# The scheduler's times come from the timeline simulation; the traced program stays the same

## The chip, the cores and the metric

One core of a Trainium2 chip runs the kernel. The metric is the device time of one launch in microseconds. Before the change the median of three runs is 2724.34 us, the lowest 2723.51 and the highest 2725.11.

A core has engines with in-order instruction streams of their own: PE (TensorE, matmuls, with a second stream for loading weights, PEld), DVE (VectorE), ACT (ScalarE), POOL (GpSimd) and SP, which here issues DMAs. They meet at semaphores. Matmuls write into PSUM, which this kernel divides into eight banks of 128 x 512 fp32.

## What is computed

A decoder trunk of four layers over 512 tokens of 1024 channels, all in fp32. Layer i has a token mixer (Gated DeltaNet, HGRN2, GLA, Gated DeltaNet) and a SwiGLU channel mixer:

```
for i in range(DEPTH):                       # DEPTH = 4
    kind, j = i % N_MIXERS, i // N_MIXERS
    if kind == 0:   m = gated_deltanet(x, gdn_w_in[j], ..., gdn_w_out[j])
    elif kind == 1: m = hgrn2(x, hgrn_w_in[j], lb_all[i], hgrn_norm_w[j], hgrn_w_out[j])
    else:           m = gla(x, gla_w_in[j], ..., gla_w_out[j])
    x = layer_norm(DN_ALPHA * x + m, mix_ln_g[i], mix_ln_b[i])
    x = layer_norm(DN_ALPHA * x + swiglu(x, ffn_w_in[i], ffn_w_down[i]), ffn_ln_g[i], ffn_ln_b[i])
```

Each mixer projects x (`x @ w_in`), runs a chunked linear recurrence over the tokens for each head (8 heads of 128 in GDN and HGRN2; 4 heads of 128 keys and 256 values in GLA), normalizes, gates and projects back. GDN has a causal convolution over 4 tokens, L2-normalized q and k, and a triangular solve in each chunk; HGRN2 and GLA have a decay for each key channel, which the kernel builds up level by level.

## The kernel before, in words

Channels lie on the 128 partitions and the 512 tokens along the free axis. A projection makes 128 channels by 512 tokens: eight blocks of 128 input channels, each with three matmuls of 512 columns (`mm3`, L183 to L185), since every fp32 operand is split into a high and a low part. The tiles are called pj (projection), vp (a block of values by tokens) and dn (output and down projections). Weights come by DMA (wraw); ACT casts the high part (whi, L144) and DVE subtracts it for the low one (wlo, L147). There are six buffers each for whi and wlo: a cast waits until the matmuls of six splits earlier have read theirs. Four PSUM banks (`acc`) take projections, four (`mx`) everything else.

The mixers add many small steps, in which one engine waits for another:

- GDN, `gdn` from L552: per half of the heads, decays (gb, L650 to L657), then for each pair of heads the projections of q and k, the convolution (`conv`, a scaling on ACT at L627, three multiply-adds on DVE at L631; for the first pair it reads a copy `raw`, for the second the PSUM bank of pj itself), silu on ACT (L637), products of k with k and q (kk, L689), transposes (tp, L505), squares on ACT (L702). Then `solve` (L820 to L909), which inverts the triangular blocks from 16 to 32 to 64 and 128 rows: L859 and L865, L877 and L891, L902 and L908 are its matmuls, with copies and transposes on ACT and DVE between; then four steps of the state (ch, L776 to L794).
- HGRN and GLA: `decay_head` (L944) builds a head's matrix am by levels. Two calls of `quad` (matmuls sc at L927) are followed by three levels of 16, 32 and 64 tokens: matmuls (L965), copies into am on ACT (L967), and two products on DVE (L972, L973) that give the next level its q and k. Then transposes (tp), a copy kt, and `decay_chains` (L983): state products su (L990), outputs ob (L995, L1003).
- `finish` normalizes a group of heads by the squares that ACT sums (L513), with the small DVE operations of `rsqrt` (L135 to L139) and a product (L533); `flush` transposes it for the output projection (ytp, L543) and multiplies by the gate (L550).

The code writes these steps down in an order that already weaves small steps with projections. The order on each engine is then made by the framework's scheduler when the program has been traced: it goes through time, and at each moment gives every engine the instruction that stands first in the traced order among those whose inputs and buffers are ready. When something is ready follows from times that the scheduler has for each instruction. Only two parts set PE's order by hand: the loading of x, and the layer norm behind a projection (`down_norm`, L355). The changed line is in `kernel`, where the context is made in which `trunk` is traced.

## Time and profile before

| | |
|---|---|
| median of three runs | 2724.34 us (2723.51 to 2725.11) |
| the profiled execution's own time | 2725.05 us |
| its span | 2723.3 us |
[...]
| instructions | 37712 |
| busy: PE, DVE, ACT, POOL | 2664.1, 1520.1, 1060.2, 90.3 us |
| read from HBM, written | 240.61 MB, 8.39 MB |

A row of a group of instructions has the line, engine, operation and tiles, the count, the busy time and the mean in ns of one, and the idle time of the engine just before them with what ended it. A PE busy time overlaps from one matmul to the next, so the spacing of matmuls is read from the number in a stretch rather than from the mean of one. An fp32 matmul of small tiles has two records, a transpose one.

### The profile page before, as it was taken

How to read it: one execution, taken by the hardware profiler on the slowest of the kernel's cores; microseconds unless marked ns; L12 is line 12 of the kernel's file. 1: busy time of each engine (PE TensorE's matmuls, PEld its weight loads, DVE VectorE, ACT ScalarE, POOL GpSimd, SP SyncE). 2: the span in 40 equal slices, each digit the busy share in tenths (PEclk: the TensorE clock that was granted, in tenths of full speed). 3: DMA queues.
4: the chain of work that ended last, by engine and by line, in shares of the span. 5: the costliest groups of instructions: out<-in, count | busy, mean ns of one | idle time of the engine just before them, and what ended most of it. 6: DMA issues, size and time to landing. Idle time of an engine off the chain costs nothing.

```text
span 2723.3 us, 37712 instructions
## 1 busy us (share of the span) xinstructions
PE 2664.1 (98%) x15279; PEld 2224.7 (82%) x15279; DVE 1520.1 (56%) x3155; ACT 1060.2 (39%) x2123; POOL 90.3 (3%) x176
## 2 busy tenths in 40 slices
PE   9999999999999999999999999999999999999998
PEld 8787888888877778888887878888887887888886
DVE  7676653333777786323366676323378586833235
ACT  5464442122544434222254634222255554422220
POOL 1000000001000000000000000000010100000000
PEclk9999999999999999999999999999999999999999
DMA  5213223223221332223321332232322132322321
GB/s 158 63 48 101 86 94 108 93 93 109 93 78 47 97 120 93 93 98 103 110 95 63 96 122 93 93 104 97 109 94 78 48 101 78 101 93 93 99 87 62
DMA packets 199678, 251.43 MB, mean 92 GB/s; under 512 B 9082, under 2 KB 152576, under 8 KB 199504
## 3 DMA queue, kind: packets, MB, share of 16 engines
q1 hardware_dynamic: 195152, 237.29, 27.1%
q0 software_dynamic: 4352, 11.73, 1.5%
q8 instruction: 120, 1.97, 0.3%
q14 instruction: 54, 0.44, 0.1%
HBM read 240.61 MB, written 8.39 MB: 91 GB/s over the span
## 4 chain that ended last, share of the span: by engine, by line
PE 81%; DVE 12%; ACT 4%; issue 2%; DMA 1%; POOL 0%; SPq 0%; DVEq 0%; ACTq 0%; POOLq 0%
PE pj L183 16%; PE pj L184 16%; PE pj L185 16%; PE dn L183 7%; PE dn L184 7%; PE dn L185 7%; DVE am L932 2%; DVE wlo L147 1%; ACT junk L702 1%; PE sc L965 1%; PE kk L689 1%; DVE qk L631 1%; PE xtp L221 1%; PE vp L183 1%; PE vp L184 1%
## 5 line engine op out<-in xcount | busy, mean ns | idle before, releaser
L183 PE MATMUL pj<-xTl,whi 128*128 128x512 f32 (+1 forms) x2472 | 925.9, 375 | 0.0
L184 PE MATMUL pj<-xTh,whi 128*128 128x512 f32 (+1 forms) x2472 | 922.3, 373 | 0.0
L185 PE MATMUL pj<-xTh,wlo 128*128 128x512 f32 (+1 forms) x2472 | 922.1, 373 | 0.0
L144 ACT CAST whi<-wraw 128x1024 fp32r<-128x1024 f32 x400 | 420.1, 1051 | 1179.4 <-PE pj L184 796.1
L147 DVE TENSOR_TENSOR wlo<-wraw,whi 128x1024 fp32r<-128x1024 f32 x400 | 487.9, 1222 | 633.5 <-ACT whi L144 633.2
L183 PEld LDWEIGHTS pj<-xTl,whi 128*128 128x128 f32 x2472 | 468.6, 190 | 78.0 <-issue 0.7
L185 PEld LDWEIGHTS pj<-xTh,wlo 128*128 128x128 f32 x2472 | 468.2, 189 | 77.7 <-issue 0.5
L184 PEld LDWEIGHTS pj<-xTh,whi 128*128 128x128 f32 x2472 | 468.5, 190 | 77.0 <-issue 0.7
L453 DVE TENSOR_TENSOR sg<-sg,pj 128x512 f32<-128x512 f32 x88 | 60.5, 687 | 247.4 <-PE pj L185 247.0
L183 PE MATMUL dn<-wlo,hhi 128*128 128x512 f32 x416 | 161.8, 389 | 0.0
L184 PE MATMUL dn<-whi,hhi 128*128 128x512 f32 x416 | 161.8, 389 | 0.0
L185 PE MATMUL dn<-whi,hlo 128*128 128x512 f32 x416 | 161.8, 389 | 0.0
L352 DVE SCALAR_TENSOR_TENSOR x<-x,dn 128x512 f32<-128x512 f32 x96 | 64.5, 684 | 69.1 <-PE dn L185 69.1
L185 PEld LDWEIGHTS dn<-whi,hlo 128*128 128x128 f32 x416 | 78.1, 188 | 16.3
L183 PEld LDWEIGHTS dn<-wlo,hhi 128*128 128x128 f32 x416 | 78.1, 188 | 16.2
L184 PEld LDWEIGHTS dn<-whi,hhi 128*128 128x128 f32 x416 | 78.1, 188 | 16.2
L183 PE MATMUL dn<-wlo,nt 128*128 128x512 f32 x224 | 87.5, 390 | 0.0
L184 PE MATMUL dn<-whi,nt 128*128 128x512 f32 x224 | 87.1, 389 | 0.0
L185 PE MATMUL dn<-whi,nt 128*128 128x512 f32 x224 | 87.1, 389 | 0.0
L183 PE MATMUL dn<-wlo,xTh 128*128 128x512 f32 x192 | 77.5, 404 | 2.8 <-ACT xTh L468 2.8
L184 PE MATMUL dn<-whi,xTh 128*128 128x512 f32 x192 | 75.9, 395 | 0.0
L185 PE MATMUL dn<-whi,xTl 128*128 128x512 f32 x192 | 74.9, 396 | 0.0
(388 smaller groups left out, 3310.7 us busy)
## 6 DMA issues: line engine op xcount, KB each, us to landing
wraw<-in_ffn_w_in SPq DMA_DIRECT2D x88, 1024.0 KB, 5.1
wraw<-in_ffn_w_down SPq DMA_DIRECT2D x40, 1024.0 KB, 5.0
wraw<-in_gdn_w_in SPq DMA_DIRECT2D x32, 1024.0 KB, 5.8
wraw<-in_hgrn_w_in SPq DMA_DIRECT2D x16, 1024.0 KB, 5.8
wraw<-in_gla_w_in SPq DMA_DIRECT2D x12, 1024.0 KB, 5.2
wraw<-in_gdn_w_out SPq DMA_DIRECT2D x8, 1024.0 KB, 5.1
xd<-x SPq DMA_DIRECT2D x24, 256.0 KB, 2.0
x<-xd SPq DMA_DIRECT2D x24, 256.0 KB, 6.5
```

What stands on the lines that cost most here:

```text
L144: nc.scalar.copy(hi, raw)
L147: (eng or nc.vector).tensor_tensor(lo, raw, hi.bitcast(F32), ALU.subtract)
L183: mm(out, ah, bl, start=start, stop=False)
L184: mm(out, ah, bh, start=False, stop=False)
L185: self.last_mm = mm(out, al, bh, start=False, stop=stop).ins
L221: nc.tensor.transpose(ps[:, k], src[:, k * P:(k + 1) * P], self.ident)
L352: self.nc.vector.scalar_tensor_tensor(s, s, alpha, ps, ALU.mult, ALU.add)
L453: nc.vector.tensor_tensor(s, s, pss[2 + j], ALU.mult)
L631: V.scalar_tensor_tensor(dst[:, T - n:], ps[:, :n], wc(t), dst[:, T - n:], ALU.mult, ALU.add)
L689: mm(pk[:, i], k[:, sl], src[:, sl], start=True, stop=True)
L702: S.activation(junk, ptk[:, i], AF.Square, accum_out=ss[:, n_src, lh * NT + i:lh * NT + i + 1])
L932: V.copy_predicated(av[:, c, js], self.lmask[b][:, gs], pm[:, c, gs])
```

## The change

One argument is added. With it the scheduler takes the times by which it chooses from the timeline simulation. The traced program, its tiles, pools and operations are the same; what changes is the order of instructions on each engine, and with it which buffer is free when.

```diff
@@ -1224,7 +1224,7 @@
     out = nc.dram_tensor("out_0", (1, T, D), F32, kind="ExternalOutput").ap()
-    with tile.TileContext(nc) as tc:
+    with tile.TileContext(nc, schedule_with_timeline_sim=True) as tc:
         trunk(tc, aps, out)
     r = run_bass_kernel_spmd(nc, [arrays], core_ids=[0])
```

About 2080 of 13389 instructions of PE, 950 of 3157 of DVE and 460 of 1869 of ACT stand elsewhere among the rest. Nearly all of them are in the four mixers. In PE's order the runs of projection matmuls (pj, vp, dn) that smaller matmuls of the mixers break number 308 before and 198 after.

In the orders below the numbers behind a name tell tiles apart: whi_109 is one cast weight, kk_66 one bank.

Before, on PE, at the first pair of heads of the first GDN layer (kk, the products of k with k and q, and tp, transposes):

```order
L184 MATMUL pj_102_705<-xTh_84,whi_100_701 128x512
L689 MATMUL kk_66_553<-qk_59_507 128x128 x4
L689 MATMUL kk_67_559<-qk_55_492,qk_59_507 128x128 x4
L505 MATMUL tp_69_566<-ident_86,qk_59_507 128x128 x4
L505 MATMUL tp_74_583<-ident_86,qk_55_492 128x128 x4
L185 MATMUL pj_102_705<-xTh_84,wlo_101_703 128x512
L689 MATMUL kk_79_596<-qk_64_544 128x128 x4
L689 MATMUL kk_80_602<-qk_57_499,qk_64_544 128x128 x4
L183 MATMUL pj_102_705<-xTl_85,whi_100_701 128x512
```

After, the same place:

```order
L185 MATMUL pj_111_777<-xTh_84,wlo_110_775 128x512
L689 MATMUL kk_66_553<-qk_59_507 128x128 x4
L689 MATMUL kk_67_559<-qk_55_492,qk_59_507 128x128 x4
L505 MATMUL tp_69_566<-ident_86,qk_59_507 128x128 x4
L505 MATMUL tp_74_583<-ident_86,qk_55_492 128x128 x4
L689 MATMUL kk_79_596<-qk_64_544 128x128 x4
L689 MATMUL kk_80_602<-qk_57_499,qk_64_544 128x128 x4
L505 MATMUL tp_82_609<-ident_86,qk_64_544 128x128 x4
L505 MATMUL tp_87_626<-ident_86,qk_57_499 128x128 x4
L183 MATMUL pj_166_979<-xTl_85,whi_157_961 128x512
```

kk and tp, which stood inside the projection pj_102, now stand in one block behind all four projections of the second pair of heads (pj_98 to pj_111), with no matmul of a projection between them.

Before, on ACT, ahead of the silus (L637) that kk_66 and its neighbours need:

```order
L627 ACTIVATE qk_64_544<-raw_65_545,cw_38_405 128x512
L637 ACT_TABLE_LOAD
L637 ACTIVATE qk_55_492<-qk_55_492 128x512
L637 ACTIVATE qk_57_499<-qk_57_499 128x512
L144 CAST whi_162_971<-wraw_161_969 128x1024
L637 ACTIVATE qk_59_507<-qk_59_507 128x512
L637 ACTIVATE qk_64_544<-qk_64_544 128x512
L697 ACTIVATE kd_68_565<-tp_69_566,gcols_39_407 128x128 x2
L702 ACTIVATE junk_70_575,ssqk_53_490<-tp_69_566 128x128
```

After, the same place:

```order
L655 ACTIVATE dm_49_471<-dm_49_471 128x512
L655 ACTIVATE dm_51_481<-dm_51_481 128x512
L144 CAST whi_175_1054<-wraw_168_1010 128x1024
L637 ACT_TABLE_LOAD
L637 ACTIVATE qk_55_492<-qk_55_492 128x512
L637 ACTIVATE qk_57_499<-qk_57_499 128x512
L637 ACTIVATE qk_59_507<-qk_59_507 128x512
L637 ACTIVATE qk_64_544<-qk_64_544 128x512
L697 ACTIVATE kd_68_565<-tp_69_566,gcols_39_407 128x128 x2
```

A later weight cast (whi_175 instead of whi_162) stands ahead of the silus. It takes the buffer that whi_109 held, the weight of pj_111.

Before, on PE, in the solve of the first half of heads of the first GDN layer (iy, iu and iw are its products):

```order
L183 MATMUL pj_307_1819<-xTl_85,whi_305_1815 128x512
L184 MATMUL pj_307_1819<-xTh_84,whi_305_1815 128x512
L185 MATMUL pj_307_1819<-xTh_84,wlo_306_1817 128x512
L908 MATMUL iw_209_1490<-nt_43_448,y3_207_1479 64x64 x8
L902 MATMUL iy_211_1501<-t64_200_1375,nt_43_448 64x64 x8
```

After, the solve's last part:

```order
L505 MATMUL tp_203_1408<-ident_86,vf_195_1327 128x128 x4
L877 MATMUL iy_198_1335<-td_154_955,nt_43_448 32x32 x16
L891 MATMUL iu_197_1334<-ud_155_956,y2_196_1333 32x32 x32
L902 MATMUL iy_208_1480<-t64_199_1374,nt_43_448 64x64 x8
L908 MATMUL iw_209_1490<-nt_43_448,y3_207_1479 64x64 x8
L902 MATMUL iy_211_1501<-t64_200_1375,nt_43_448 64x64 x8
L908 MATMUL iw_212_1511<-nt_43_448,y3_210_1500 64x64 x8
L650 MATMUL gb_214_1522<-gr_42_444,sel_91 128x512
```

The projections pj_205 and pj_307 stood between L891, L902 and L908; after, the block from L877 to L908 is broken by one group of transposes only.

Before, on PE, in the second GLA head (sc, the level products; pj_1871 and pj_1884 are projections of the gate):

```order
L965 MATMUL sc_1867_12457<-qk_1785_11981,qk_1780_11948 32x32 x4
L183 MATMUL pj_1871_12476<-xTl_85,whi_1869_12472 128x512
L184 MATMUL pj_1871_12476<-xTh_84,whi_1869_12472 128x512
L965 MATMUL sc_1867_12457<-qk_1785_11981,qk_1780_11948 32x32 x4
L185 MATMUL pj_1871_12476<-xTh_84,wlo_1870_12474 128x512
L183 MATMUL pj_1884_12540<-xTl_85,whi_1882_12536 128x512
L184 MATMUL pj_1884_12540<-xTh_84,whi_1882_12536 128x512
L185 MATMUL pj_1884_12540<-xTh_84,wlo_1883_12538 128x512
L965 MATMUL sc_1873_12503<-qk_1785_11981,qk_1780_11948 64x64 x4
```

After, the same head:

```order
L927 MATMUL sc_1852_12350<-wq_1850_12337,qk_1780_11948 128x192 x2
L995 MATMUL ob_1827_12252<-nt_1786_11983,am_1787_11984 128x128
L1003 MATMUL ob_1827_12252<-Sst_1842_12299,qk_1781_11950 128x128
L927 MATMUL sc_1856_12372<-wq_1855_12368,qk_1780_11948 128x192 x2
L927 MATMUL sc_1857_12381<-wq_1855_12368,qk_1780_11948 128x192 x2
L965 MATMUL sc_1865_12432<-qk_1785_11981,qk_1780_11948 16x16 x16
L965 MATMUL sc_1867_12457<-qk_1785_11981,qk_1780_11948 32x32 x8
L965 MATMUL sc_1873_12503<-qk_1785_11981,qk_1780_11948 64x64 x4
L505 MATMUL tp_1876_12514<-ident_86,qk_1780_11948 128x128 x4
L543 MATMUL ytp_1877_12520<-ident_86,on_1828_12253 128x128 x4
L543 MATMUL ytp_1879_12527<-ident_86,on_1829_12254 128x128 x4
L990 MATMUL su_1891_12599<-nt_1786_11983,kt_1875_12513 128x128 x3
```

From the last L927 products to the state products su (L990) no projection is left between; in the first GLA head, 20 to 25 of them stand between two groups of L965 where 2 stood before. At the ends of the mixers, 26 (GDN), 35 (HGRN) and 69 (GLA) matmuls of the output projection stood between the last small product and the transposes ytp of L543; after, none.

## Rows read from the trace of the kernel before

**Rows 1.** page, part 1 (busy time of PE) and part 4 (chain, by engine)

```profile
PE 2664.1 (98%) x15279; PEld 2224.7 (82%) x15279; DVE 1520.1 (56%) x3155; ACT 1060.2 (39%) x2123; POOL 90.3 (3%) x176
...
PE 81%; DVE 12%; ACT 4%; issue 2%; DMA 1%; POOL 0%; SPq 0%; DVEq 0%; ACTq 0%; POOLq 0%
```

**Rows 2.** waits of PE: engine, line, releaser; us in total, times, longest

```profile
PE iy L859 <- DVE td L849: 6.3, 4, 1.8
PE dn L183 <- DVE yy L550: 4.8, 1, 4.8
...
PE kk L689 <- ACT qk L637: 3.3, 6, 0.8
...
PE sc L965 <- DVE qk L939: 0.2, 1, 0.2
```

**Rows 3.** stretches: an FFN, a GDN solve, the last mixer's output projection

```profile
core 0: us, PE busy (x) PEld busy (x) DVE busy (x) ACT busy (x) POOL busy (x), PEclk, DMA share, GB/s
480.00:548.00 68.00, 68.00 (x302) 56.31 (x301) 22.07 (x23) 14.22 (x14) 0.00 (x0) 1.00 0.28 93
...
112.00:119.00 7.00, 6.91 (x115) 5.62 (x115) 1.90 (x3) 0.63 (x1) 2.98 (x6) 0.53 0.02 5
...
2312.00:2316.00 4.00, 2.72 (x6) 1.86 (x7) 3.79 (x7) 1.24 (x2) 1.28 (x3) 0.67 0.40 101
```

**Rows 4.** groups by line, 30 to 75 us (first GDN layer, front part)

```profile
L147 DVE TENSOR_TENSOR wlo<-wraw,whi 128x1024 fp32r<-128x1024 f32 x8 | 9.7, 1217 | 0.6 <-ACT whi L144 0.6
L631 DVE SCALAR_TENSOR_TENSOR qk<-raw,cw,qk 128x511 f32<-128x511 f32 (+2 forms) x12 | 9.7, 874 | 0.0
L144 ACT CAST whi<-wraw 128x1024 fp32r<-128x1024 f32 x8 | 8.4, 1050 | 4.2 <-PE pj L184 2.9 <-issue 1.3
L631 DVE SCALAR_TENSOR_TENSOR qk<-pj,cw,qk 128x511 f32<-128x511 f32 (+2 forms) x11 | 8.2, 745 | 2.1 <-ACT qk L627 1.9
...
L637 ACT ACTIVATE qk<-qk 128x512 f32<-128x512 f32 x7 | 4.3, 627 | 0.6 <-DVE qk L631 0.5
...
L138 DVE SCALAR_TENSOR_TENSOR rsq<-rsq,sse 128x16 f32<-128x16 f32 x3 | 0.5, 175 | 0.1
```

**Rows 5.** groups by line, 100 to 150 us (GDN solve)

```profile
L895 DVE COPY nt<-iu 32x512 f32<-32x512 f32 x2 | 1.4, 684 | 1.7 <-PE iu L891 1.7
...
L903 ACT COPY y<-iy 64x512 f32<-64x512 f32 x2 | 1.2, 581 | 3.1 <-PE iy L902 3.1
...
L894 DVE STREAM_TRANSPOSE t<-iu 32x256 f32<-32x256 f32 x2 | 0.8, 418 | 0.0
```

**Rows 6.** timeline of DVE, second GLA head: start, us, engine, line, operation

```profile
1465.29 0.69 DVE L953 TENSOR_REDUCE dg<-tp 128x4 f32<-128x512 f32 x1 [1.23 <-PE tp L505]
...
1474.27 0.55 DVE L939 TENSOR_TENSOR qk<-qk,sx 128x384 f32<-128x384 f32 x1
...
1479.98 0.42 DVE L972 TENSOR_TENSOR qk<-qk,pt 128x256 f32<-128x256 f32 x1 [3.59 <-PE sc L965]
1480.32 0.42 DVE L973 TENSOR_TENSOR qk<-qk,pt 128x256 f32<-128x256 f32 x1
```

**Rows 7.** timeline of PE, the same head

```profile
1465.57 1.47 PE L927 MATMUL sc<-wq,qk 128*128 128x192 f32 x8
...
1475.10 0.36 PE L965 MATMUL sc<-qk,qk 128*16 128x16 f32 x8
...
1485.85 0.60 PE L505 MATMUL tp<-ident,qk 128*128 128x128 f32 x4
```

**Rows 8.** groups by line, 1455 to 1500 us (GLA)

```profile
L513 ACT ACTIVATE junk<-on 128x128 f32<-128x128 f32 x12 | 3.7, 309 | 0.3
...
L513 ACT ACTIVATION_READ_ACCUMULATOR junk<-on 128x1 f32 x12 | 2.3, 188 | 0.0
L965 PEld LDWEIGHTS sc<-qk,qk 128*16 128x16 f32 (+2 forms) x56 | 2.2, 105 | 2.5 <-issue 1.4 <-ACT am L967 1.1
...
L533 DVE TENSOR_TENSOR on<-on,occ 128x512 f32<-128x512 f32 x2 | 1.3, 688 | 0.0
```

## The prediction

> **What bounds the kernel now.** I read the page first, then the waits of PE, then stretches of the mixers. PE is busy 98% of the span and carries 81% of the chain that ended last; DVE and ACT follow with 12% and 4% [rows 1]. The reader should take from this that PE's own list of matmuls is the kernel, and that only what stands between two matmuls can change. In a stretch of an FFN nothing stands there: 302 matmuls fill 68.00 of 68 us, a spacing of 0.225 us, with DVE at a third [rows 3]. All named waits of PE, 18 rows in the view, add up to 48.3 us; the first and the last are shown [rows 2]. Nearly all lie in the mixers (GDN, HGRN, GLA, GDN), where small matmuls wait for DVE or ACT and the scheduler lays projection matmuls between them as fill. About 14.8 us of the 48.3 lie where the change moves nothing (the loading of x and the output projections, the 4.8 us of dn behind yy among them), so 33.5 us can go at most by removed waits.

> **What the change moves.** No instruction is added or taken away. FFN, output projections and norms keep their order on PE; the mixers change. Runs of projection matmuls that are broken by small ones fall from 308 to 198. The new order gives early small steps much more fill than they need (about 20 projection matmuls between two L965 groups in the first GLA head, where 2 stood), and the fill is then missing later: whole chains of dependent small steps stand with nothing between them. I price these bare places one by one: the time that DVE and ACT need from the last matmul before the gap to the one behind it, less the PE work that still stands between.

> *GDN, front part.* After: kk_66 stands right behind the last matmul of pj_111. On ACT the cast whi_175 now stands ahead of the four silus; it takes the buffer of whi_109, which pj_111's last matmuls read. On DVE its subtract stands ahead of two conv products that the silu of qk_59 needs. The chain is cast 1.05, subtract 1.22, two products 0.87 each, silu 0.63, with handovers of about 0.2: 4.8 us, with one matmul beside it [rows 4]. Before, kk_66 stood amid pj_102, behind casts whose buffers were long free. Next: the following projection needs an acc bank, free when the conv of pj_98 has run. After, DVE has seven products that read pj directly (0.745 each, 5.2 us) ahead of that release, behind the transposes that it follows, and PE has 0.44 us left to do: 5 us with the handover [rows 4]. In the second half of heads the same release comes again, 5 us, and 1 us at the transposes ahead of it. Sum 16 us a layer, 32 us for two.

> *GDN solve.* L877, L891, L902 and L908 stand in one block. L891's second half waits for two transposes and a copy on DVE (2 x 0.42 + 0.68 + 0.15 = 1.7); each L908 for ACT's copy (0.58 + 0.2 = 0.8, twice); the second y2 copy and the first state step for about 0.7 each: 4.6 us [rows 5]. The second half of heads loses the fill between L865 and L877 as well (2.6 more): 7.2. Sum 12 a layer, 24 for two.

> *Mixer ends.* Before, 26 to 69 matmuls (6 to 15 us at 0.225) stand between the last small matmul of a mixer and the transposes ytp (L543); now none. The chain there is a copy and a square of ACT (0.31 each, the copy is no longer) with its read-out 0.19, about 12 DVE operations of 0.175, a product of 0.69, and 0.6 of handovers: 4.2 us [rows 4, 8]. Four mixers: 17.

> *GLA.* Heads 2 and 4 are bare from their transposes tp to the state products su. Before, DVE's part of that takes from 1465.29 to 1474.82, 9.5 us, and L965 starts at 1475.10 [rows 6, 7]. After, four pairs of L927 matmuls (1.47 for two pairs) and eight ob (two passes of 0.11 each, by four transposes in 0.60, rounded down for the overlap) stand in it, 4.9 us; 4.6 stay open [rows 7]. Then three levels with nothing between, 0.42 + 0.34 + a handover of 0.25 = 1.0 each [rows 6]. 7.6 a head, 15 for two; head 3 has bare levels and a bare L990, 4. Sum 19.

> *HGRN.* Two heads alternate, so a level's 1.0 lies partly beside the other head's matmuls. Level by level, 18 short places of 0.5 to 1.0 us in four pairs: 11.

> *Clock.* [...] It also falls once outside the solves, right behind the 4.8 us wait of dn for yy [rows 2]: 0.67 in the 4 us from 2312, so 2.7 us at half clock in that stretch, 1.3 lost at least [rows 3]. That wait is as long as the gaps that I price above, so falls will come behind some of them. Bounds are none and one at each of the 16 barest places (two kk, four releases, four solve tails, four ends, two GLA heads) at 2.8: 0 to 45. I take a third of that, 15 us: the solves have their fall already, and a gap is often cut by small matmuls.

> *Gains.* Removed waits: 0 to 33.5. Since the early chains now have fill to spare I take 33. Fewer changeovers: weight loads sit idle 2.5 us ahead of seven L965 groups, 0.36 each [rows 8]; elsewhere a changeover shows nothing. With 110 fewer the bounds are 0 and 40; I take 0.2 each, 22.

> *Sum.* 32 + 24 + 17 + 19 + 11 + 15 = 118 lost, 55 gained: +63 on the profiled execution's own 2725.05 us, 2788. The median of the runs shown is 0.7 below that execution, so 2787.

> **Rivals.**
> [...]
> *It becomes faster.* The price of a bare place is an upper bound where DVE or ACT had got ahead while PE waited at the place before. In this rival half of the 103 us of bare places is hidden so (the second release in GDN behind the wait at kk, levels of GLA beside late quads), no further fall of the clock comes, and the gains come in full (33 and the upper 40): 52 - 73 = -21, 2704. With the gains at 55 it decides once less than 55 of the 103 us are real. For it speaks that DVE is busy only 56% and ACT 39% [rows 1], so neither is behind on the whole; against it that at each place named the chain starts at a matmul that ends right before the gap.
> *It does nothing.* PE's work is the same and a wait may only change place: 2725. For it: the PE share of 98% and the untouched FFN [rows 1, 3]. Against: losses and gains would have to cancel within 6 of 118 us.

> **How the numbers follow.** The forecast 0.58, the clock 0.20, faster 0.13, nothing 0.09. The forecast's own range, with one GDN term gone or the clock's term gone at one end and the gains halved at the other, is 2755 to 2815. For eight in ten I reach beyond the clock's case above and nearly to no change below: 2730 to 2835, with 0.13 left below and 0.07 above. A measurement of this kernel tells about 0.2%, 5.4 us, from no change. Faster by more than that 0.15 (its rival and a fifth of nothing), within it 0.05, slower 0.80.

> **What the profile after would show.** Waits of PE at kk L689 for ACT's silu of some 4 us, once a GDN layer, a granted clock of half behind some of them; a wait of a projection L183 for DVE L631 of some 5 us, twice a layer; iu L891 for DVE, iw L908 for ACT's L903; ytp L543 for DVE L533 of some 4 us in each mixer; sc L965 for DVE in GLA. The waits iy L859 and tp L505 for qk should be gone or small, and FFN stretches should still hold 302 matmuls in 68 us. I am wrong if PE's named waits do not at least double from 48 us, or if they do and the idle of weight loads shrinks by as much.

## The result and the profile after

The changed kernel takes 2877.16 us (median of four runs, 2871.68 to 2878.69) against 2724.73 us of the kernel before, also four runs: a ratio of 1.0556 with a 95% interval of 1.0539 to 1.0573. Slower was forecast, but 2787 us, and the range ended at 2835. The profiled execution took 2871.68 us, with a span of 2870.0 us against 2723.3.

The page's parts 1 and 4 after, which answer to [rows 1]: busy time, and the chain by engine.

```profile
PE 2712.1 (94%) x15279; PEld 2285.9 (80%) x15279; DVE 1511.6 (53%) x3155; ACT 1059.6 (37%) x2123; POOL 88.2 (3%) x176
...
PE 87%; DVE 9%; ACT 3%; issue 1%; DMA 0%; SPq 0%; DVEq 0%; ACTq 0%
```

The instructions are the same in number, but PE is busy 48 us longer: the same matmuls ran slower, which fits the clock in the stretches below and its mean over the span, 0.962 of full speed where 0.993 stood. The other 99 us of the longer span are idle time of PE. Here are its waits after, to be held against [rows 2]: engine, line, releaser; us in total, times, longest.

```profile
PE pj L183 <- DVE qk L631: 20.1, 6, 5.1
PE ytp L543 <- DVE on L533: 18.3, 5, 4.7
PE kk L689 <- ACT qk L637: 13.9, 2, 7.6
PE xtp L221 <- ACT x L403: 13.3, 7, 4.3
PE pj L183 <- DVE xTl L234: 7.4, 7, 1.5
PE sc L965 <- DVE k L973: 6.9, 8, 1.5
PE iu L891 <- DVE nt L895: 6.6, 4, 1.7
PE iw L908 <- ACT y L903: 5.8, 8, 0.7
PE sc L965 <- ACT am L967: 5.6, 12, 1.0
...
PE dn L185 <- DVE xTl L469: 4.8, 2, 2.6
```

All rows of the view add up to 145.2 us where 48.3 stood. Row by row, 31.1 us went (iy L859, 6.3, and tp L505 for qk L950, 4.4, are gone) and 128.0 came. Stretches show what the clock did, beside [rows 3]: an FFN, the wait at kk, and one stretch in the solve of each half of the first GDN layer's heads.

```profile
527.00:595.00 68.00, 68.00 (x302) 56.33 (x301) 22.03 (x23) 14.22 (x14) 0.00 (x0) 1.00 0.28 93
68.50:75.50 7.00, 3.82 (x18) 3.82 (x19) 3.76 (x5) 3.69 (x5) 0.00 (x0) 0.54 0.55 151
157.50:174.50 17.00, 14.95 (x111) 12.68 (x109) 8.57 (x25) 7.03 (x13) 3.79 (x7) 0.51 0.08 27
301.00:325.00 24.00, 18.44 (x233) 17.27 (x233) 6.92 (x12) 6.53 (x14) 2.97 (x6) 0.50 0.07 22
```

The spacings of PE's records, each against its usual length at full clock, can be summed in three parts. Gaps of over 0.5 us grew by 105 us in all, the other spacings at half clock by 64, and the small gaps at full clock shrank by 21. That is 148 of 147 us, to the rounding; other limits between the parts move each of them by up to some 10 us. By stages, each cut behind the same number of matmuls in both kernels (us):

| stage | before | after | difference | half clock before | after |
|---|---|---|---|---|---|
| GDN fronts, two | 151.3 | 176.2 | +24.9 | 0.0 | 27.4 |
| GDN solves and states, two | 411.9 | 472.6 | +60.7 | 27.8 | 108.2 |
| HGRN | 265.2 | 266.6 | +1.4 | 0.0 | 20.4 |
| GLA | 186.0 | 215.2 | +29.2 | 0.0 | 36.1 |
| output projections and norms, four | 188.6 | 220.7 | +32.1 | 2.8 | 19.6 |
| FFNs and the rest | | | -1.7 | 7.2 | 5.4 |

The profiled execution is the shortest of the four, and HGRN's +1.4 is at the low end: in the profiles of five other kernels below that have HGRN in this same order (hgrn_after, norm_before, gdn_before, gdn_before2, gla_before) it took 269.3 to 273.9 us, with 27 to 31 us at half clock.

The wait that was forecast first, kk L689, on PE after: start, us, engine, line, operation, and in brackets the idle time before it and its releaser.

```profile
63.71 0.39 PE L185 MATMUL pj<-xTh,wlo 128*128 128x512 f32 x1
71.68 2.08 PE L689 MATMUL kk<-qk 128*128 128x128 f32 x8 [7.58 <-ACT qk L637]
...
79.25 0.66 PE L505 MATMUL tp<-ident,qk 128*128 128x128 f32 x4 [0.31 <-ACT junk L702]
85.03 0.77 PE L183 MATMUL pj<-xTl,whi 128*128 128x512 f32 x1 [5.13 <-DVE qk L631]
85.60 0.63 PE L184 MATMUL pj<-xTh,whi 128*128 128x512 f32 x1
```

And ACT in the same stretch:

```profile
63.91 1.04 ACT L144 CAST whi<-wraw 128x1024 fp32r<-128x1024 f32 x1 [3.34 <-PE pj L184]
68.53 1.28 ACT L637 ACT_TABLE_LOAD   x1 [3.57 <-DVE qk L631]
69.82 2.47 ACT L637 ACTIVATE qk<-qk 128x512 f32<-128x512 f32 x4
```

And DVE:

```profile
64.59 1.21 DVE L147 TENSOR_TENSOR wlo<-wraw,whi 128x1024 fp32r<-128x1024 f32 x1
65.73 2.72 DVE L631 SCALAR_TENSOR_TENSOR qk<-raw,cw,qk 128x510 f32<-128x510 f32 x4
68.37 1.21 DVE L147 TENSOR_TENSOR wlo<-wraw,whi 128x1024 fp32r<-128x1024 f32 x1
69.51 2.06 DVE L631 SCALAR_TENSOR_TENSOR qk<-raw,cw,qk 128x509 f32<-128x509 f32 x3
```

The cast stands ahead of the silus as the order had shown, but it isn't what is late. It ends at 64.95, and its subtract starts at 68.37, 3.4 us later: DVE, without a gap, works on an earlier subtract and four products until then. Two more products follow, until 70.90. ACT waits for the last of those four, and then a table load of 1.28 us and two earlier silus, until 70.97, stand ahead of the silu that kk_66 needs. The two paths end together; the forecast's chain had neither DVE's queue ahead of the subtract nor the table load. The projection that follows waits 5.13 us (forecast: 5) and its first matmuls show 0.63 us where 0.39 is usual, a start every 0.43 us.

### The profile page after: what moved, and what is told of

Its sections match the earlier page's. It is cut to its first block, busy times and chain, and to the rows that moved or that the text cites. A ratio compares the mean times of both kernels' runs of the same rounds, so it can differ in the third digit from the quotient of the medians.

```text
span 2870.0 us, 37723 instructions
## 1 busy us (share of the span) xinstructions
PE 2712.1 (94%) x15279; PEld 2285.9 (80%) x15279; DVE 1511.6 (53%) x3155; ACT 1059.6 (37%) x2123; POOL 88.2 (3%) x176
## 4 chain that ended last, share of the span: by engine, by line
PE 87%; DVE 9%; ACT 3%; issue 1%; DMA 0%; SPq 0%; DVEq 0%; ACTq 0%
PE pj L183 17%; PE pj L184 17%; PE pj L185 17%; PE dn L185 7%; PE dn L183 7%; PE dn L184 7%; DVE qk L631 1%; PE tp L505 1%; PE kk L689 1%; PE sc L927 1%; PE sc L965 1%; PE xtp L221 1%; DVE x L256 1%; PE vp L183 1%; PE vp L184 1%
## 5 line engine op out<-in xcount | busy, mean ns | idle before, releaser
L183 PE MATMUL pj<-xTl,whi 128*128 128x512 f32 (+1 forms) x2472 | 923.9, 374 | 27.5 <-DVE qk L631 20.1
L185 PE MATMUL pj<-xTh,wlo 128*128 128x512 f32 (+1 forms) x2472 | 918.8, 372 | 0.1
L183 PEld LDWEIGHTS pj<-xTl,whi 128*128 128x128 f32 x2472 | 467.9, 189 | 108.1 <-issue 10.7
L185 PEld LDWEIGHTS pj<-xTh,wlo 128*128 128x128 f32 x2472 | 467.4, 189 | 79.1 <-issue 0.4
L183 PE MATMUL dn<-wlo,hhi 128*128 128x512 f32 x416 | 161.8, 389 | 0.0
L185 PE MATMUL dn<-whi,hlo 128*128 128x512 f32 x416 | 161.4, 390 | 0.0
L352 DVE SCALAR_TENSOR_TENSOR x<-x,dn 128x512 f32<-128x512 f32 x96 | 64.9, 684 | 70.1 <-PE dn L185 70.1
L185 PEld LDWEIGHTS dn<-whi,hlo 128*128 128x128 f32 x416 | 78.1, 188 | 16.3
L183 PEld LDWEIGHTS dn<-wlo,hhi 128*128 128x128 f32 x416 | 78.1, 188 | 16.1
L183 PE MATMUL dn<-wlo,nt 128*128 128x512 f32 x224 | 87.5, 390 | 0.0
L185 PE MATMUL dn<-whi,nt 128*128 128x512 f32 x224 | 85.3, 389 | 0.0
L183 PE MATMUL dn<-wlo,xTh 128*128 128x512 f32 x192 | 76.2, 398 | 0.0
L185 PE MATMUL dn<-whi,xTl 128*128 128x512 f32 x192 | 69.9, 401 | 4.8 <-DVE xTl L469 4.8
```

The costliest lines, as they stand in the source:

```text
L183: mm(out, ah, bl, start=start, stop=False)
L185: self.last_mm = mm(out, al, bh, start=False, stop=stop).ins
L352: self.nc.vector.scalar_tensor_tensor(s, s, alpha, ps, ALU.mult, ALU.add)
```

## The experiments

The account that the runs came to: each stage pays for its own order, on all engines together, in waits of PE and the half clock behind them. The expectations name the theories as they stood at each run. In the first two, Theory A says that PE's own order carries the loss, and Rival B that the order on DVE and ACT does. Later Theory A is that each stage pays for its own order, and B that its cost comes from, or moves to, what stands around it. In the runs on the clock, A says that half clock comes from PE's standing still ahead of it, and C that it comes from the sparse small matmuls themselves.

Most kernels here fix an engine's order by a list of instruction numbers, which are the same in both programs:

```diff
     with tile.TileContext(nc) as tc:
         trunk(tc, aps, out)
+        pin(nc, tc)
+def pin(nc, tc):
...
+            if prev is not None:
+                tc.add_manual_dep(i, prev.name, mybir.DependencyInfo(
+                    mybir.DependencyClass.NoSync, mybir.DependencyReason.DATA), reason="pin")
+            prev = i
```

### One engine's order: pe_before and pe_after

pe_before keeps the changed call (`schedule_with_timeline_sim=True`) and lists only PE's order, that of before; pe_after is the kernel before with only PE's new order listed. The scheduler places the other engines' instructions around it.

> Times from the timeline simulation as in the changed kernel, but PE's matmuls are held in the order of the kernel before; DVE, ACT, POOL and SP are ordered by the scheduler. Theory A (PE's order, with its bare places, carries the loss; what remains is the norm's order on DVE and ACT, some 20 us): 2745 us, within 2730 to 2760, named waits of PE under 75 us, under 60 us at half clock. Rival B (the order on DVE and ACT makes PE late, wherever its matmuls stand): 2840 or more, waits over 130.

> The scheduler's usual times as in the kernel before, but PE's matmuls are held in the order of the changed kernel. Theory A: 2855 us, within 2835 to 2875, since the bare places are back and only the norm's part of some 20 us is not. Rival B (DVE and ACT): 2750 or less.

Measured: pe_before 2803.78 us (1.0288, 1.0273 to 1.0303), half clock 95 us; pe_after 2860.04 us (1.0498, 1.0482 to 1.0514), half clock 218 us. The first lies between both theories, the second in A's range; so PE's order alone doesn't carry the loss. With PE's old order the new times still cost 80 us, in waits for DVE and ACT, which were ordered by them. The waits of PE in pe_before:

```profile
PE iy L859 <- DVE td L849: 15.4, 4, 4.5
PE kk L689 <- ACT qk L637: 11.5, 6, 2.6
PE xtp L221 <- ACT x L403: 10.5, 10, 2.3
PE dn L185 <- DVE xTl L469: 7.3, 2, 6.2
```

iy L859 stood 6.3 us before [rows 2]. The two halves, 80 and 136 us, are more than the 152 of both: an order of one engine is good or bad only against the orders of the others.

### The norms: norm_before and norm_after

norm_before is the kernel after with the four stretches behind the mixers (the end of the output projection and the layer norm) listed in the order of before on every engine; norm_after is the kernel before with the order of after in them.

> All engines in the order of the changed kernel, except that in the layer norms behind the four mixers' output projections DVE, ACT and PE have the order of before. The four norm stages took 32 us longer after the change. Theory A (the order of the norm's small steps on DVE and ACT, which lets PE's transposes xtp wait for L403): 2857 us, within 2850 to 2865, and the wait of xtp for L403 falls from 13.3 us to under 4. Rival (the norm is late because the mixer before it ends bare and late, whatever the order in it): 2874 or more and the wait stays over 10.

> The kernel before, with only the four stretches of the layer norms behind the mixers in the order of after on every engine; all mixers and FFNs as before. In the kernel after these four stretches grew by 3.1 + 10.6 + 12.1 + 6.3 = 32 us. Theory A (the norms' own order is what costs there, most of all the norm chains of two row tiles interleaved on DVE, for which PE's transposes stand 13.3 us): most of the 32 us comes, 2745 us or more. Rival B (the mixers in front end late and hand it on, as the run with the norms put back, -9 us, and the run with HGRN alone in the new order, +4 us in its norm, suggest): the norms' own part is 9 to 17 us, 2734 to 2742 us, with an xtp wait of some 13 us.

Measured: norm_before 2867.77 us (1.0528, 1.0511 to 1.0546), 9 us below after, between the two expectations; its xtp wait is gone, but dn L185 for xTl L469 rose from 4.8 to 10.3 us and half clock to 239 us. norm_after 2746.57 us (1.0083, 1.0066 to 1.0100): +22 us by these stretches alone, as Theory A had it. Its waits of PE:

```profile
PE xtp L221 <- ACT x L403: 12.5, 4, 4.3
PE pj L183 <- DVE xTl L234: 7.4, 7, 1.5
```

PE keeps its order there, but for 11 to 24 matmuls at a place, two places a norm, that alternate otherwise between banks. DVE after, behind HGRN:

```profile
1052.91 0.74 DVE L550 SCALAR_TENSOR_TENSOR y<-ytp,cw,zg 128x512 f32<-128x512 f32 x1
1053.57 1.28 DVE L257 TENSOR_TENSOR x<-x,lnp 128x512 f32<-128x512 f32 x2
1054.77 0.74 DVE L550 SCALAR_TENSOR_TENSOR y<-ytp,cw,zg 128x512 f32<-128x512 f32 x1
1055.43 3.69 DVE L257 TENSOR_TENSOR x<-x,lnp 128x512 f32<-128x512 f32 x6
1059.05 1.28 DVE L469 TENSOR_TENSOR xTl<-y,xTh 128x512 fp32r<-128x512 f32 x2
...
1072.92 0.35 DVE L389 SCALAR_TENSOR_TENSOR lnc<-lnc 128x1 f32<-128x1 f32 x2
...
1074.28 0.16 DVE L398 SCALAR_TENSOR_TENSOR lnc<-lnc 128x1 f32<-128x1 f32 x1
```

PE in the same stretch:

```profile
1059.78 1.20 PE L185 MATMUL dn<-whi,xTl 128*128 128x512 f32 x4 [2.60 <-DVE xTl L469]
1075.02 1.64 PE L221 MATMUL xtp<-ident,x 128*128 128x128 f32 x8 [4.28 <-ACT x L403]
```

Six norm products stand ahead of the low half xTl that PE needs, and the small chains of two row tiles run interleaved, so that the first ends nearly as late as the second. Cut behind the same number of matmuls, the four norm stretches take 3.1, 8.1, 7.1 and 5.4 us more in norm_after than before, and give back 3.2, 3.7, 7.1 and 0.1 in norm_before. So the norms of HGRN and of the last GDN layer stay late there with their own order put back. That mixers which end late hide part of the norms' cost fits this, but no run shows it by itself.

### Stage by stage: gdn_before, gdn_before2, gla_before, hgrn_after

The same lists, cut by stage: the kernel after with the GDN layers, or GLA, in the order of before; the kernel before with HGRN in the order of after. In gdn_before, PE's part of the second GDN front stayed in the new order by a wrong cut; gdn_before2 has the whole.

> The kernel after, with the two GDN layers (fronts and solves) put back into the order of before on every engine; HGRN, GLA and the norms keep the new order. Theory A (each stage pays for its own waits and its own half clock): the six GDN stretches grew by 13.2 + 14.1 + 17.2 + 11.7 + 14.9 + 14.5 = 85.6 us, all of it comes back: 2791 us (2783 to 2800), half clock about 100 us instead of 217. Rival B (as in the run with the norms put back, where of 16 us of waits only 9 came back): the waits move to the borders of the stretches, the time stays over 2815 us.

> As the run with the two GDN layers put back, with the one thing mended that was left out there: TensorE's order in the front of the second GDN layer had stayed that of after, against DVE and ACT in the order of before, and stood 9.4 us for one silu. Theory A (each stage pays for its own): the 85.6 us by which the six GDN stretches grew come back whole: 2791 us (2784 to 2798), half clock 120 us or less. Rival B (waits move to the borders): 2803 us or more.

> The kernel after, with the GLA mixer alone put back into the order of before on every engine. Theory A (each stage pays for its own): GLA grew from 186.0 to 215.2 us, so 2877 - 29 = 2848 us (2842 to 2855), half clock 217 - 34 = 183 us. Rival B (the late end moves into the norm behind it): 2860 us or more.

> The kernel before, with the HGRN mixer alone in the order of after on every engine. Theory A: in the kernel after that mixer took 262.2 us against 261.6, its 9.9 us of saved changeovers paying for its waits and its 21 us of half clock: 2726 us (2721 to 2731), half clock 38 + 21 = 59 us. Rival B (the mixer's order leaves the norm behind it late, +10 us there): 2734 us or more. Rival C (without the disturbed stages around it the changeovers are a gain): 2717 us or less.

Measured: gdn_before 2809.35 us (1.0317, 1.0301 to 1.0332), gdn_before2 2791.78 (1.0245, 1.0229 to 1.0261), half clock 119 us; gla_before 2843.48 (1.0437, 1.0422 to 1.0453), half clock 198 us where 183 was expected; hgrn_after 2739.12 (1.0049, 1.0033 to 1.0066). The GDN layers give back 85.4 of their 85.6 us. Cut at the same DVE instructions, the stretches put back take 75.8, 139.8 and 64.1 us in gdn_before2 against 75.8, 140.0 and 64.1 before: what stands around a GDN layer does not change it. GLA gives back 34, with the norm behind it in part. HGRN costs 14 alone: B has that number but not its place, since by the same cut 10 us are in the mixer, where B had none, and 4 in the norm behind it, where it had 10. The missed cut is instructive: with only PE in the new order the second front took 92.3 us against 75.7, more than the 90.0 by the same cut with all engines in it. The wait of gdn_before there:

```profile
PE kk L689 <- ACT qk L637: 13.7, 6, 9.4
```

One stage at a time, the costs are 85 (GDN), 34 (GLA), 14 (HGRN) and 22 (norms): 155 of 152 us. That it fits so well is partly luck: two are costs taken away and two are costs put in, and GLA's and HGRN's count some of the norms behind them, 4 to 5 us each by the cuts used here, a second time.

### The clock: warm, warm_before, warm_all

warm is the kernel after with 208 matmuls at four kinds of waits, into banks that the next matmuls overwrite:

```diff
+    def warm(self, out, n):
+        x = self.xT[0][:, KD - 1]
+        for _ in range(n):
+            self.extra.add(self.nc.tensor.matmul(out, x[:, :P], x[:, :out.shape[1]], start=True, stop=True).ins.name)
...
+                        if h == 0 and src is k:
+                            self.warm(pk.rearrange("p c t -> p (c t)"), 24)
```

warm_before is the kernel before with matmuls of zeros (24 columns wide) in the solves' waits:

```diff
         pu = py[:, 1]
+        self.warm(py.rearrange("p a h c -> p (a h c)"), 7)
         with self.behind(filled):
...
+        self.warm(pu.rearrange("p h c -> p (h c)"), 11)
         for i in range(hc):
```

warm_all is warm with such zeros everywhere, and in the solves at L865, L891 and L908 as well.

> All engines in the order of the changed kernel, with 208 matmuls added whose results are overwritten, at places where PE waits: 24 ahead of the first kk of each GDN layer, 16 ahead of the last transposes before the wait for an acc bank (four places), 16 ahead of the first ytp of each mixer's end, 16 short ones ahead of the first L965 of GLA heads 2 and 4. They add some 44 us of PE work inside waits. [...] Rival C (the falls come with the small matmuls, not with the waits): half clock stays over 200 and the time at 2870 to 2890.

> The kernel before in its own order, with 72 matmuls of zeros put in front of the first and the second group of 16x16 matmuls of each of the four solves (7 of 512 and 11 of 256 columns), where PE waits 1.4 to 1.8 us and then about 1 us, so that PE works while it waits. Nothing that is computed changes. Theory A (the four stretches of 6.8 us at half clock, which begin about 5 us after those waits, are made by the standing still): half clock 38 falls to about 11 us and the time by some 9 us, to 2715 us (2708 to 2721). Rival C (they come from the sparse small matmuls that follow, not from the waits): half clock over 30 us and 2723 to 2732 us.

> The kernel after in its own order, with matmuls that change nothing put where PE stands: at the four places of the earlier run (208, now matmuls of zeros) and in the four solves, where PE has only the 16x16 to 64x64 matmuls (84 more: 8 before the second group of 16x16, 7 before the 32x32 of L891, 3 before each group of L908). Theory A (the long stretches of 17 and 24 us at half clock in the solves are made by standing still between small matmuls, and half clock costs some 0.3 to 0.45 us a us, as in the kernel before with its four stretches filled): half clock 163 falls to 70 to 100 us, the time from 2864 to about 2838 us (2830 to 2850). Rival C (the solves' half clock does not go by filling, or costs nothing since the solves wait for DVE anyway): 2857 us or more.

Measured: warm 2864.19 us (1.0513, 1.0497 to 1.0529), half clock 163 us where 217 stood, named waits 42 us fewer: against C, which named over 200 us at half clock and 2870 us or more; warm_before 2715.74 (0.9969, 0.9957 to 0.9980), half clock 17 us, as A had it; warm_all 2887.11 (1.0594, 1.0579 to 1.0609), half clock 160 us, far from A and in the range that C named. PE in warm, at the place that was shown of after (its lines stand 7 to 12 further down, L83 are the added matmuls):

```profile
62.84 5.60 PE L83 MATMUL kk<-xTh 128*128 128x512 f32 x24
70.58 1.16 PE L701 MATMUL kk<-qk 128*128 128x128 f32 x8 [2.14 <-ACT qk L647]
...
77.24 3.90 PE L83 MATMUL tp<-xTh 128*128 128x512 f32 x16
80.98 0.60 PE L513 MATMUL tp<-ident,qk 128*128 128x128 f32 x4
82.99 0.47 PE L190 MATMUL pj<-xTl,whi 128*128 128x512 f32 x1 [1.41 <-DVE qk L641]
83.30 0.39 PE L191 MATMUL pj<-xTh,whi 128*128 128x512 f32 x1
```

kk starts as late after the last projection as in after, 7.6 us from its end to the first kk: that wait belongs to ACT and DVE. But the projection behind the second wait starts at once at 0.39 us a matmul. In both GDN fronts together half clock falls from 27 to 3 us, and they get 3.1 and 3.6 us shorter: 0.28 us for each us at half clock. Over the whole kernel it is 13 us for 54, 0.24. In warm_before the fill pays as much: the stretch behind the first solve's waits (0.53 in [rows 3]) is at full clock,

```profile
110.50:117.50 7.00, 6.41 (x155) 5.02 (x154) 4.00 (x6) 0.70 (x2) 2.63 (x5) 1.00 0.01 2
```

and the four stretches of 27 us at half clock are gone, for which the solves together are 8.4 us shorter: 0.31 us a us. So these four stretches go when PE doesn't stand still ahead of them, and C falls for these places. In the solves of after, C can't be dismissed. There 84 more fillers left 92 us at half clock, where warm without them had 86 and after 108, and the four solves took 7.6, 5.1, 4.5 and 5.2 us longer than in warm, nearly all of the 23 us between the two kernels. PE in warm_all, in the first solve:

```profile
155.97 1.19 PE L909 MATMUL iu<-ud,y 32*32 32x32 f32 x32
158.81 1.28 PE L909 MATMUL iu<-ud,y 32*32 32x32 f32 x32 [1.65 <-DVE nt L913]
160.02 1.97 PE L920 MATMUL iy<-t,nt 64*64 64x64 f32 x16
161.91 1.47 PE L83 MATMUL iw<-xTh,nil 128*24 128x512 f32 x3
163.31 1.65 PE L927 MATMUL iw<-nt,y 64*64 64x64 f32 x13
```

The wait of 1.65 us was not filled, since that bank holds results by then, and the clock fell behind it as before; the fillers that follow, at half clock, take 0.47 us each and add more than the 0.7 us waits that they cover. What the half clock in these solves costs by itself stays open.

### A faster version: best

best is warm_before with one swap on DVE. Behind the second GDN mixer eight norm products, 5 us, stand ahead of the gate product that PE waits 4.8 us for in the kernel before [rows 2]:

```diff
-L256 L256 L257 L257 L256 L256 L257 L257 L550 L256 L550 L469 L257 L469
+L550 L550 L469 L469 L256 L256 L257 L257 L550 L256 L256 L257 L257 L469
```

> The kernel before with its solve waits filled (the 72 matmuls of zeros, 2715.7 us), and one more edit: behind the second GDN mixer two gate products (L550) and two low halves (L469) go ahead of the eight layer-norm products (L256, L257, 5 us) that stand before them in DVE's queue; all other engines as before. Theory A (an in-order queue: PE's wait of 4.8 us for that product is the norm work ahead of it, and the half clock of 6.8 us after it comes from the wait): the wait goes, half clock 17 falls to about 10 us, 2710 us (2706 to 2713). Rival B (the norm work is late next, at the drains L352 or the next xTl): 2714 us or more.

Measured: 2715.95 us (0.9963, 0.9949 to 0.9977), the same as warm_before: rival B. The wait and its fall of the clock are gone (half clock 11 us), and the time is given back behind them. Waits of PE in best:

```profile
PE xtp L230 <- ACT x L412: 4.0, 5, 2.4
...
PE dn L194 <- DVE xTl L478: 1.6, 2, 1.2
```

xtp had 1.6 us in warm_before. DVE is busy 6.90 of 7 us there,

```profile
2294.00:2301.00 7.00, 6.84 (x36) 5.03 (x35) 6.90 (x13) 2.29 (x3) 0.00 (x0) 1.00 0.00 0
```

and by this row the norm can't end much before DVE has done all of it: PE's wait was where DVE's work came to light, not what cost the time. By the count of matmuls, the stretch up to the output projection is 4.7 us shorter than in warm_before, and the one behind it 4.9 us longer. Both versions beat the kernel before by 0.3 to 0.4%.

## Why the prediction was right in direction and too small

- **The bare places of the mixers: right.** They were priced at 103 us. The new waits are 128.0 us, of which the rows of the norms and of the output projections' xTl (xtp L221 for L403, pj L183 for L234, dn L185 for L469) are 23.9, and 2.4 more are at the loading of x: 102 in the mixers. By group, with the forecast in brackets: GDN fronts with the releases 34 (32), solves 19 (24), mixer ends 18 (17), GLA 21 (19), HGRN 10 (11). So the total is closer than its parts, which miss by up to 5 us both ways. Single prices hold as well: the release L183 20.1 us of all rows for four of 5, ytp L543 18.3 for four of 4.2, iu L891 1.65 for 1.7, iw L908 0.72 for 0.8. Only kk was too small, 7.6 and 6.3 us for 4.8 twice: the chain lacked DVE's queue ahead of the subtract, and ACT's table load of 1.28 us with the silus in front.
- **The gains: near.** 31.1 us of waits went for 33, but 6.0 of them (dn L183 for yy and xTh, pj L197) at the output projections and the loading of x, where none was expected; the small gaps at full clock shrank by 21 us for 22, by the cut above.
- **"FFN, output projections and norms keep their order on PE", and so cost nothing: wrong.** This step failed. PE's order was kept but for neighbours, DVE's and ACT's was not, and PE waits for them there. It cost 24 us of new waits, 32 us in the stages, and 22 us alone in norm_after.
- **The clock: mis-sized.** This term failed most: 15 us were taken, a third of "one at each of the 16 barest places" at 2.8 us, and PE's spacing at half clock grew by 64. No run shows a loss of 2.8 us a place; what the runs show is 11 us at half clock a place, and 0.24 to 0.31 us for each us of it. Every one of the 16 places has its stretch at half clock in the profile after, 177 us in all or 11 us each, where a loss of 2.8 us means 5.6; seven more stretches lie in HGRN, GLA and the norms. So the places were counted right, taking a third of them was wrong, and the stretches are longer than priced. Five of the six that last 14 to 24 us begin in or behind waits of 1.4 to 2.7 us, in the solves' tails and in GLA, and go on through the small matmuls and short waits that follow. "The solves have their fall already" was the wrong reason to take a third: after, they hold half of all half clock, 108 of 217 us.
- **The sum** with the measured terms: 128 + 64 - 31 - 21 = +140 of the +147 that the profiled executions differ by; with the forecast's it was +63. The two wrong terms make 73 of the 77 between. The terms come from two ways of cutting, waits and spacings, and the last 7 us stay open.
- **The rivals.** The clock's case, with a chance of 0.20, had one of the two terms that failed: its upper bound of 45 us in the place of 15 would make 2817 us, still too small. A stretch stands at each of the 16 places as that bound counts them, but the stretches are longer, and it had no norms. Half clock rose from 37.9 to 217.1 us with the waits, though the longest stretches, 17 and 24 us, begin in or behind waits of 1.4 to 2.7 us. And the runs put its net price below the 64 us: 6.7 us for 24 in the fronts, 8.4 for 27 in the solves of before, 13 for 54 in warm. At these 0.24 to 0.31 us a us, 179 us would be 43 to 56 us, an estimate. "It becomes faster" by chains that are partly hidden is refuted by the 102 of 103 us. "It does nothing" too.

All the signs that were named for the profile after were there. Why the simulated times choose an order with fill early and none later no run here shows.

## What to carry to other kernels

A change to a scheduler's times must be read on every engine's queue, also where the bounding engine's own order stays: here DVE's queue, worked off in its order, made PE wait where hardly a matmul had moved, 22 us in norm_after. Price each new wait by its chain, with what stands ahead in each engine's queue; here that came within 5 us a group of places. Then count the clock by the stretches of small matmuls behind the waits, not by the number of long waits: here waits of 1.4 to 2.7 us stood at the start of the longest stretches, 17 and 24 us. A wait of the bounding engine need not be worth its length: best removed one of 4.8 us and gained nothing, with DVE, which had released it, busy for 6.90 of 7 us there.

## What the runs showed of the hardware

- In the first GDN layer's solves of after the granted clock was 0.51 and 0.50 of full speed over 17 and 24 us while PE was busy 14.95 and 18.44 us of them, mostly in matmuls of 16 to 64 rows and columns. A wait of 1.65 us ended just ahead of the first, and the second began within one of 2.64 us.
- In warm_before, matmuls of zeros, 24 columns wide, stood in waits of 0.6 to 1.8 us. Half clock was 17 us where 37.9 stood, the four stretches of the solves were gone (a granted clock of 1.00 in the 7 us where 0.53 stood), and the kernel was 0.3% faster (ratio 0.9957 to 0.9980).
- Half clock cost less than half of its time: 24 us less of it made the two GDN fronts 6.7 us shorter (warm against after), 27 us less the four solves 8.4 us (warm_before against before).
